# Pool columns of the input projection: one 512- and one 256-column product per block instead of three of 256

## The chip, the cores and the metric

The kernel runs on one core of a Trainium2 chip. The metric is the device time of one execution in microseconds; the median of three runs is compared.

## The reference

One layer of a decoder trunk on 256 tokens of width 2048, all in float32. Cut to what matters here:

```
h   = rmsnorm(x)
z   = h @ w_in          # pool channels (1024) | q | k | v | indexer q | indexer k | indexer weights
A   = pool_mixer(u_pool)        # 4 groups of 256 channels, causal means over 2/4/8/16 tokens
B   = dsa_attention(q, k, v, q_idx, k_idx, w_idx)     # 64 best keys per query, softmax attention
x1  = x + concat(A, B) @ w_out
out = x1 + conv_ffn(rmsnorm(x1))

pool_mixer:  d = (mean over the last w tokens) - u, for each group
             y = (d @ pool_w[group]) * pool_scale
```

## The kernel before

Every float32 number that TensorE multiplies is split in two: a high half (the value rounded to TensorE's format) and a low half (what is left). A product of two float32 matrices is then high x high, high x low and low x high, and low x low is left out. The tile xhl holds the normalised input, feature by feature, as [128, block, half, 256 tokens], so high and low half of one block lie side by side; whi and wlo hold the two halves of 1024 weight columns of the 128 partitions.

The work is a list of *pieces*, each of them 1024 weight columns: a DMA on SyncE's queue brings a unit of two pieces (tile raw), ScalarE rounds to whi (L103), VectorE subtracts to wlo (L104), TensorE runs the piece's products. There are four buffers of whi and of wlo, so a piece's split waits for the piece four earlier. The pieces come in the order of ORDER: the indexer chunks (24 pieces), k0 and k1, u0, q0 and q1, u1, v0, u2, v1, u3, then the output projection (32), the up projection (176) and the down projection (88). A chunk u0 to u3 is a pool chunk: four pieces, for two tiles of 128 pool columns, and its window is 16, 8, 4 and 2 in that order.

There are three forms of product in which the weights are stationary and 256 tokens move. With a rhs of both halves, mm_feat (L216, L217) streams high and low half in one product of 512 columns against whi, and the high half once more against wlo; its accumulator has 512 columns, and low half's sum lies in columns 256 to 511. mm_feat1 (L221 to L223) runs three products of 256 columns that all add into columns 0 to 255. The up projection and most of the down projection use mm_feat; pool chunks, the pool mixer, the output projection and the last two tiles of the down projection use mm_feat1. The query, key, value and indexer chunks use the other form, mm_tok (L210 to L212), with the weights moving.

Accumulators of a chunk come from a pool of two, each of two banks of 512 columns; a chunk holds its accumulator from its first product until it has been taken out.

Work beside the pieces is hung on steps of the list with at(step, ...): at a step, first the split of the piece two further on, then the side work of the step, then the products of the step's own piece. For pool chunk n with its first piece at step f, the weights of the mixer are loaded and split at f - 2 and f + 2, pool_u (L541 to L545) takes the accumulator out at f + 4, pool_win (L547) computes the window sums on VectorE and the two halves dhl (ScalarE L566, VectorE L567), and pool_mix multiplies by pool_w. For the first three chunks pool_win hangs on step f + 5 and pool_mix on f + 10; for the last on f + 4 and f + 6. So between the last chunk and its mixer TensorE has two pieces of the output projection and two attention outputs (L529, L530, taken out by L531 and L532). The framework's planner sets the final order on each engine: instructions come in the order of the program, but one that is ready in the planner's own times can go ahead of one that is not.

The up projection's accumulators are taken out by up_out (L635 to L637): ScalarE copies the columns 256 to 511, VectorE adds the columns 0 to 255 and multiplies by the token norm.

Of the kernel before, what the change touches and what calls it, by code (L numbers as in the profile page):

```python
# [11 lines left out]
AF = mybir.ActivationFunctionType  # L12
ALU = mybir.AluOpType
AX = mybir.AxisListType

P = 128
S = 256
D = 2048
KT = D // P
# [24 lines left out]
def hybrid_kernel(ctx, tc, xT, par, wIa, wIb, wIc, wI2, wA, wU, wP, wO, wUp, wDn, out):  # L44
    nc = tc.nc
# [9 lines left out]
    xhl = cp.tile([P, KT, 2, S], F32R, name="xhl")  # L55
# [114 lines left out]
    r1, r2 = TokenNorm("r1"), TokenNorm("r2")  # L170
# [43 lines left out]
    def mm_feat(o, wh, wl, rhs, first, last):  # L214

        nc.tensor.matmul(o, wh, rhs.rearrange("p a t -> p (a t)"), start=first, stop=False)  # L216
        nc.tensor.matmul(o[:, 0:S], wl, rhs[:, 0], start=False, stop=last)  # L217

    def mm_feat1(o, wh, wl, rhs, first, last):

        nc.tensor.matmul(o[:, 0:S], wh, rhs[:, 0], start=first, stop=False)  # L221
        nc.tensor.matmul(o[:, 0:S], wh, rhs[:, 1], start=False, stop=False)  # L222
        nc.tensor.matmul(o[:, 0:S], wl, rhs[:, 0], start=False, stop=last)  # L223
# [13 lines left out]
    def pool_chunk(n):  # L237
        acc = Acc()
        for j in range(2):
            u = Unit(wU[2 * n + j], D)  # L240
            for h in range(2):
                def mm(p, j=j, h=h):
                    pt = acc.get()
                    for i in range(8):
                        k = 8 * h + i
                        mm_feat1(pt[:, j], *p.get(i * P, P), xhl[:, k], k == 0, k == KT - 1)
                pieces.append(Piece(u, h * 1024, (h + 1) * 1024, mm))
        return acc

# [287 lines left out]
    def wide(name):  # L537
        return zc.tile([P, 2, S + 16], F32, name=name, tag="t2", bufs=5)

    def pool_u(n):  # L540
        pt = ua[n].get()  # L541
        ub = wide("ub")
        nc.gpsimd.memset(ub[:, :, 0:16], 0.0)
        nc.vector.tensor_tensor(ub[:, :, 16:], pt[:, :, 0:S], r1.b2(), op=ALU.mult)
        pw_[n] = ub  # L545

    def pool_win(n):  # L547
# [161 lines left out]
    for n in range(4):  # L709
        st = first[f"u{n}"] + 4  # L710
        at(st, pool_u, n)
        at(st - 6, pool_w, n)
        at(st - 2, pool_ws, n)
        at(st + (n < 3), pool_win, n)
        at(st + 2 + 4 * (n < 3), pool_mix, n)
# [112 lines left out]
```

## Time and profile before

| | us |
|---|---|
| median of three runs | 1098.67 (1098.51 to 1098.75) |
| the profiled execution | 1098.5 |
| its span in the trace | 1096.8 |
| TensorE busy | 1090.8 |
| VectorE busy | 729.8 |
| ScalarE busy | 569.7 |

The span runs from the first to the last instruction in the trace, and the profiled execution took 1.7 us more than its span. Engines are listed with the time in which at least one of their instructions ran. TensorE's matmuls overlap, and their ends are modelled, so the distance between two starts tells more of a product than its listed duration. A weight split is one ScalarE instruction of about 1.06 us and one VectorE instruction of about 1.23 us.

### The profile page before, as it was taken

How to read it: one execution, taken by the hardware profiler on the slowest of the kernel's cores; microseconds unless marked ns; L12 is line 12 of the kernel's file. 1: busy time of each engine (PE TensorE's matmuls, PEld its weight loads, DVE VectorE, ACT ScalarE, POOL GpSimd, SP SyncE). 2: the span in 40 equal slices, each digit the busy share in tenths (PEclk: the TensorE clock that was granted, in tenths of full speed). 3: DMA queues.
4: the chain of work that ended last, by engine and by line, in shares of the span. 5: the costliest groups of instructions: out<-in, count | busy, mean ns of one | idle time of the engine just before them, and what ended most of it. 6: DMA issues, size and time to landing. Idle time of an engine off the chain costs nothing.

```text
span 1096.8 us, 16441 instructions
## 1 busy us (share of the span) xinstructions
PE 1090.8 (99%) x6620; PEld 973.5 (89%) x6620; DVE 729.8 (67%) x1037; ACT 569.7 (52%) x796; POOL 13.8 (1%) x25
## 2 busy tenths in 40 slices
PE   9999999999999999999999999999999999999998
PEld 7988889889999888888888888888888888888898
DVE  7667857665565687777777777777787544444442
ACT  7555456654444555555555555555555443333441
POOL 0001000000000000000000000000000000000000
PEclk9999999999999999999999999999999999999999
DMA  8554564444555555555555555555555556555552
GB/s 289 169 188 148 178 231 156 164 163 154 171 180 189 192 192 192 189 184 192 186 189 183 191 191 192 188 192 192 192 192 192 193 201 201 197 195 198 195 197 74
DMA packets 31755, 204.30 MB, mean 186 GB/s; under 512 B 3648, under 2 KB 4288, under 8 KB 8640
## 3 DMA queue, kind: packets, MB, share of 16 engines
q1 hardware_dynamic: 30240, 201.16, 53.7%
q10 hardware_dynamic: 1440, 2.11, 0.5%
q8 instruction: 52, 0.85, 0.3%
q14 instruction: 23, 0.19, 0.0%
HBM read 201.15 MB, written 2.10 MB: 185 GB/s over the span
## 4 chain that ended last, share of the span: by engine, by line
PE 99%; DMA 1%; SPq 0%; ACT 0%; DVE 0%; issue 0%; ACTq 0%
PE mm L216 43%; PE mm L217 21%; PE mm L210 5%; PE mm L212 5%; PE mm L211 5%; PE mm L221 5%; PE mm L222 5%; PE mm L223 5%; PE sp L403 1%; DMA xf<-in_xT_dram 1%; PE sp L489 0%; PE tp L477 0%; PE op L529 0%; PE tp L517 0%; PE tp L393 0%; PE pm L221 0%
## 5 line engine op out<-in xcount | busy, mean ns | idle before, releaser
L104 DVE TENSOR_TENSOR wlo<-raw,whi 128x1024 fp32r<-128x1024 f32 (+4 forms) x385 | 462.6, 1203 | 296.2 <-ACT whi L103 294.9
L103 ACT ACTIVATE whi<-raw 128x1024 fp32r<-128x1024 f32 (+4 forms) x385 | 399.9, 1041 | 429.4 <-PE mm L216 262.4
L216 PE MATMUL mm<-xhl,whi 128*128 128x512 f32 x1408 | 488.4, 394 | 0.0
L217 PE MATMUL mm<-xhl,wlo 128*128 128x256 f32 x1408 | 390.1, 277 | 0.0
L216 PEld LDWEIGHTS mm<-xhl,whi 128*128 128x128 f32 x1408 | 264.0, 187 | 61.0
L217 PEld LDWEIGHTS mm<-xhl,wlo 128*128 128x128 f32 x1408 | 264.4, 188 | 0.0
L216 PE MATMUL mm<-ghl,whi 128*128 128x512 f32 x616 | 213.6, 394 | 0.0
L217 PE MATMUL mm<-ghl,wlo 128*128 128x256 f32 x616 | 170.6, 277 | 0.0
L216 PEld LDWEIGHTS mm<-ghl,whi 128*128 128x128 f32 x616 | 115.5, 188 | 26.8
L217 PEld LDWEIGHTS mm<-ghl,wlo 128*128 128x128 f32 x616 | 115.7, 188 | 0.0
L210 PE MATMUL mm<-whi,xhl 128*128 128x512 f32 (+3 forms) x288 | 108.3, 376 | 1.1 <-ACT xhl L120 0.5
L212 PE MATMUL mm<-whi,xhl 128*128 128x512 f32 (+3 forms) x288 | 106.8, 371 | 0.0
L211 PE MATMUL mm<-wlo,xhl 128*128 128x512 f32 (+3 forms) x288 | 106.6, 370 | 0.2 <-DVE wlo L104 0.2
L221 PE MATMUL mm<-yhl,whi 128*128 128x256 f32 x256 | 72.2, 282 | 0.0
L223 PE MATMUL mm<-yhl,wlo 128*128 128x256 f32 x256 | 72.1, 281 | 0.0
L222 PE MATMUL mm<-yhl,whi 128*128 128x256 f32 x256 | 72.1, 281 | 0.0
L210 PEld LDWEIGHTS mm<-whi,xhl 128*128 128x128 f32 x288 | 54.1, 188 | 9.0 <-issue 0.9
L212 PEld LDWEIGHTS mm<-whi,xhl 128*128 128x128 f32 x288 | 54.1, 188 | 8.3 <-DVE xhl L123 0.5
L211 PEld LDWEIGHTS mm<-wlo,xhl 128*128 128x128 f32 x288 | 54.1, 188 | 7.3 <-DVE wlo L104 0.4
L654 ACT ACTIVATE ghl<-fc 128x256 fp32r<-128x256 f32 x44 | 18.4, 417 | 57.8 <-DVE fc L653 57.8
L221 PEld LDWEIGHTS mm<-yhl,whi 128*128 128x128 f32 x256 | 48.2, 188 | 0.0
L222 PEld LDWEIGHTS mm<-yhl,whi 128*128 128x128 f32 x256 | 48.2, 188 | 0.0
(156 smaller groups left out, 955.6 us busy)
## 6 DMA issues: line engine op xcount, KB each, us to landing
raw<-in_wUp_dram SPq DMA_DIRECT2D x88, 1024.0 KB, 4.8
raw<-in_wDn_dram SPq DMA_DIRECT2D x44, 1024.0 KB, 4.8
raw<-in_wA_dram SPq DMA_DIRECT2D x24, 1024.0 KB, 4.8
raw<-in_wO_dram SPq DMA_DIRECT2D x16, 1024.0 KB, 4.8
raw<-in_wU_dram SPq DMA_DIRECT2D x8, 1024.0 KB, 5.0
raw<-in_wI_dram SPq DMA_DIRECT2D x4, 640.0 KB, 4.0
raw<-in_wIb_dram SPq DMA_DIRECT2D x3, 784.0 KB, 4.5
xf<-in_xT_dram SPq DMA_DIRECT2D x8, 256.0 KB, 4.9
```

Source lines behind the costliest of these rows:

```text
L103: i1 = nc.scalar.activation(hi, raw, AF.Copy)
L104: i2 = nc.vector.tensor_tensor(self.lo[:, c:c + n], raw, hi.bitcast(F32), op=ALU.subtract)
L210: nc.tensor.matmul(o, xhl[:, k, 0, t], wh, start=(k == 0), stop=False)
L211: nc.tensor.matmul(o, xhl[:, k, 0, t], wl, start=False, stop=False)
L212: nc.tensor.matmul(o, xhl[:, k, 1, t], wh, start=False, stop=(k == KT - 1))
L216: nc.tensor.matmul(o, wh, rhs.rearrange("p a t -> p (a t)"), start=first, stop=False)
L217: nc.tensor.matmul(o[:, 0:S], wl, rhs[:, 0], start=False, stop=last)
L221: nc.tensor.matmul(o[:, 0:S], wh, rhs[:, 0], start=first, stop=False)
L222: nc.tensor.matmul(o[:, 0:S], wh, rhs[:, 1], start=False, stop=False)
L223: nc.tensor.matmul(o[:, 0:S], wl, rhs[:, 0], start=False, stop=last)
L403: nc.tensor.matmul(sp[:, a:b], q, kiT[:, e, 0:b - a], start=(e == 0), stop=(e == 1))
L654: nc.scalar.activation(ghl[:, f, 0], c[:, 0], AF.Copy)
```

## The change

The pool chunks call mm_feat in place of mm_feat1, so a block takes one product of 512 and one of 256 columns, and the accumulator has the low half's sum in columns 256 to 511. pool_u therefore has two more instructions ahead of the multiplication by the token norm: ScalarE copies the columns 256 to 511 into the tile ub, and VectorE adds the columns 0 to 255 to it; the multiplication then works on ub in place.

```diff
@@ -243,7 +243,7 @@
                     pt = acc.get()
                     for i in range(8):
                         k = 8 * h + i
-                        mm_feat1(pt[:, j], *p.get(i * P, P), xhl[:, k], k == 0, k == KT - 1)
+                        mm_feat(pt[:, j], *p.get(i * P, P), xhl[:, k], k == 0, k == KT - 1)
                 pieces.append(Piece(u, h * 1024, (h + 1) * 1024, mm))
         return acc
 
@@ -541,7 +541,10 @@
         pt = ua[n].get()
         ub = wide("ub")
         nc.gpsimd.memset(ub[:, :, 0:16], 0.0)
-        nc.vector.tensor_tensor(ub[:, :, 16:], pt[:, :, 0:S], r1.b2(), op=ALU.mult)
+        uv = ub[:, :, 16:]
+        nc.scalar.activation(uv, pt[:, :, S:2 * S], AF.Copy)
+        nc.vector.tensor_tensor(uv, pt[:, :, 0:S], uv, op=ALU.add)
+        nc.vector.tensor_tensor(uv, uv, r1.b2(), op=ALU.mult)
         pw_[n] = ub
```

## Rows read from the trace of the kernel before

**Rows 1.** The page: busy time by engine, granted TensorE clock, chain that ended last.

```profile
PE 1090.8 (99%) x6620; PEld 973.5 (89%) x6620; DVE 729.8 (67%) x1037; ACT 569.7 (52%) x796; POOL 13.8 (1%) x25
...
PEclk9999999999999999999999999999999999999999
...
PE 99%; DMA 1%; SPq 0%; ACT 0%; DVE 0%; issue 0%; ACTq 0%
```

**Rows 2.** Busy time by stretch: stretch, its us, each engine's busy us, clock, DMA.

```profile
8.90:1093.30 1084.40, 1084.24 (x6600) 970.51 (x6600) 725.80 (x1029) 565.74 (x790) 12.05 (x14) 1.00 0.55 186
...
123.45:139.00 15.55, 15.55 (x71) 12.88 (x70) 13.57 (x18) 6.55 (x7) 0.00 (x0) 1.00 0.57 201
```

**Rows 3.** Products by line: count, ns (least/median/most), first and last start, forms.

```profile
L216 PE MATMUL mm<-xhl,whi x1408: 391/392/476, 359.1 to 847.7; 128*128 128x512 f32 x176
...
L216 PE MATMUL mm<-ghl,whi x616: 392/394/395, 848.1 to 1061.3; 128*128 128x512 f32 x154
...
L221 PE MATMUL mm<-yhl,whi x256: 279/281/363, 265.7 to 358.7; 128*128 128x256 f32 x128
...
L221 PE MATMUL mm<-ghl,whi x88: 280/283/283, 1061.6 to 1092.9; 128*128 128x256 f32 x88
...
L221 PE MATMUL pm<-dhl,pwh x16: 279/283/283, 139.8 to 273.3; 128*128 128x256 f32 x16
```

**Rows 4.** TensorE in order of time around the first pool chunk: start, us, instruction.

```profile
111.72 0.39 PE L212 MATMUL mm<-whi,xhl 128*128 128x512 f32 x1
111.94 0.28 PE L221 MATMUL mm<-xhl,whi 128*128 128x256 f32 x1
...
123.45 0.40 PE L210 MATMUL mm<-whi,xhl 128*128 128x512 f32 x1
```

**Rows 5.** Groups by line and form: count, busy us, mean ns, idle before.

```profile
L637 DVE TENSOR_TENSOR up<-ft,r2b 128x512 f32<-128x512 f32 x44 | 30.4, 692 | 1.5
L636 DVE TENSOR_TENSOR ft<-mm,ft 128x512 f32<-128x512 f32 x44 | 30.1, 684 | 0.0
L635 ACT ACTIVATE ft<-mm 128x512 f32<-128x512 f32 x44 | 25.4, 577 | 0.0
...
L544 DVE TENSOR_TENSOR ub<-mm,r1b 128x512 f32<-128x512 f32 x4 | 2.8, 690 | 1.6 <-PE mm L223 1.6
```

**Rows 6.** VectorE in order of time after the first pool chunk.

```profile
126.25 0.68 DVE L544 TENSOR_TENSOR ub<-mm,r1b 128x512 f32<-128x512 f32 x1
...
131.13 1.23 DVE L104 TENSOR_TENSOR wlo<-raw,whi 128x1024 fp32r<-128x1024 f32 x1 [0.92 <-ACT whi L103]
...
135.72 0.69 DVE L567 TENSOR_TENSOR dhl<-d,dhl 128x512 fp32r<-128x512 f32 x1 [0.70 <-ACT dhl L566]
```

**Rows 7.** VectorE, then ScalarE, in order of time after the last pool chunk.

```profile
265.37 0.69 DVE L544 TENSOR_TENSOR ub<-mm,r1b 128x512 f32<-128x512 f32 x1 [0.60 <-PE mm L223]
...
266.81 0.42 DVE L532 TENSOR_TENSOR yhl<-op,yhl 128x256 fp32r<-128x256 f32 x1
...
267.81 1.22 DVE L104 TENSOR_TENSOR wlo<-raw,whi 128x1024 fp32r<-128x1024 f32 x1
...
269.80 0.69 DVE L567 TENSOR_TENSOR dhl<-d,dhl 128x512 fp32r<-128x512 f32 x1 [0.70 <-ACT dhl L566]
...
265.25 1.06 ACT L103 ACTIVATE whi<-raw 128x1024 fp32r<-128x1024 f32 x1 [1.99 <-PE mm L222]
266.21 0.36 ACT L531 ACTIVATE yhl<-op 128x256 fp32r<-128x256 f32 x1
```

**Rows 8.** TensorE in order of time, from the last pool chunk past its mixer.

```profile
265.05 0.28 PE L223 MATMUL mm<-xhl,wlo 128*128 128x256 f32 x1
...
272.31 0.28 PE L222 MATMUL pm<-dhl,pwh 128*128 128x256 f32 x1
...
273.62 0.28 PE L221 MATMUL mm<-yhl,whi 128*128 128x256 f32 x1
```

**Rows 9.** Waits: engine and line, for what, us in total, times, longest us.

```profile
ACT zq L445 <- PE mm L212: 3.1, 2, 1.7
```

## The prediction

> **What bounds the kernel now.** The page comes first: busy shares, granted clock, chain of waits [rows 1]. TensorE is busy 1090.8 us of a 1096.8 us span, the chain that ended last is TensorE to 99%, and the granted clock reads full speed in all 40 slices, so the 2.4 GHz level is not at stake. Busy time can deceive, because matmuls overlap, so the second view is the busy time by stretch [rows 2]: between 8.90 and 1093.30 us TensorE leaves 0.16 us open, and the 6.0 us of idle lie nearly all at the start and the end. The kernel is a queue of products with no gap. Its time changes by what the change takes out of that queue, plus any gap that it opens; vector work counts only where it opens one.
>
> VectorE does not bound the kernel, but it is close in one of the stretches that the change touches: 13.57 us busy of 15.55 us after the first pool chunk [rows 2]. So the third view is the order of instructions around the points where a pool accumulator is taken out.
>
> **The change on TensorE.** Four pool chunks of two column tiles by 16 blocks make 128 blocks. Each now takes three 256-column products, and will take a 512- and a 256-column one. Columns stay at 768; one product, with its weight load, goes. What a product costs is the distance from start to start, not its duration, since the listed durations overlap.
> - Three products on pool blocks: the first chunk runs 32 blocks from 111.94 to 123.45 us with nothing between [rows 4], 359.7 ns each. The last stage does the same on another tile: 88 blocks with first starts from 1061.6 to 1092.9 us [rows 3], 31.3 / 87 = 359.8 ns.
> - Two products, 512 + 256: 1408 blocks of the up projection start at 359.1 us, and the next stage's first at 848.1 [rows 3], 489.0 / 1408 = 347.3 ns. The down projection, 616 blocks from 848.1 to 1061.3: 213.2 / 615 = 346.7 ns.
> - A third stage gives a lower price for three products: the output projection's last 240 blocks start from 273.62 [rows 8] to 358.7 us [rows 3], 85.1 / 239 = 356 ns.
>
> The same tile pair (xhl, whi) gives 359.7 - 347.3 = 12.4 ns a block, the final stage 359.8 - 346.7 = 13.1 ns, the cheapest triple against the dearer pair 356 - 347.3 = 8.7 ns. Times 128 that is 1.6, 1.7 and 1.1 us. I take **1.6 us off the queue**, because it is from the loop that is changed and from the form that it gets, and keep 1.1 and 1.7 as bounds. The trace has both forms at the same granted clock, so there is no reason for a value outside by the clock.
>
> **The change on ScalarE and VectorE.** Per chunk, ScalarE gains one copy out of the accumulator, the same shape as the copy in the up projection: 577 ns [rows 5]. VectorE gains one addition out of the accumulator, 684 ns, and its multiplication now reads SBUF: 692 ns against 690 ns now [rows 5], taken as nothing. So four times 0.58 us on ScalarE and 0.68 us on VectorE, and the window work of a chunk starts at least 0.58 + 0.68 = 1.26 us later. The 5.0 us of vector work are nothing if TensorE never finds a buffer empty. Chunk by chunk:
> - First chunk. VectorE reaches the multiplication at 126.25 us, 2.7 us after the chunk's last product started; that is time for the copy. The addition pushes VectorE's queue 0.68 us back, but VectorE stands idle 0.92 us for ScalarE before the split at 131.13 [rows 6], which takes that up. Cost 0; without that idle stretch it would push the end of the mixer's input from 135.72 + 0.69 = 136.41 us [rows 6] to 137.1, still ahead of the mixer's first product at 139.8 [rows 3].
> - Second and third chunk. The mixer runs six pieces after the chunk, as in the first: at least 15.8 us, a piece of 12 products being 12 times the 0.22 us that a 512-column product holds the queue [rows 4]. The chain from taking out to mixer input was 10.2 us in the first chunk (126.25 to 136.41 [rows 6]), which has the most window steps. Cost 0; the chain would have to grow by some 5 us first.
> - Last chunk. Only two pieces lie between it and its mixer, so here is **the one tight place**. The last product starts at 265.05 [rows 8]; the vector chain starts at 265.37 and ends with the mixer's low half at 269.80 + 0.69 = 270.49 [rows 7]. TensorE's first product that reads that half starts at 272.31 [rows 8]. The cover is 1.8 us against at least 1.26 us more: it holds by half a microsecond if the copy starts at once. It may not. ScalarE begins a weight split at 265.25 and follows it with an attention output [rows 7], so the copy may start near 266.5 and end near 267.05. Then VectorE would do the split and the attention subtraction first (they stand inside the chain now, at 267.81 and 266.81, 1.13 and 0.33 us of it), and the addition would start near 267.9. From there the chain is its own work: 0.65 for the addition, 0.65 multiplication, 0.7 window, 0.65 difference, 0.25 for the two fixes, 0.7 ScalarE, 0.7 the last subtraction, that is about 272.2, on the edge. One more weight split in the gap before the last subtraction (VectorE is free there for 0.7 us) makes it 273.0 and a stall of 0.7 us. The order on each engine is set by a planner, whose own times the trace does not show, so I bound the stall by 0 and 0.8 us and take **0.3 us**, nearer to the first end because only one of the orders gives it.
>
> **Buffers.** The accumulator is held 1.26 us longer or more. There are two; the next chunk has the other one, and the one after that starts eight pieces later, or four after the last chunk: from 273.62 to 265.05 [rows 8] are already 8.6 us, and the next use is later still. Cost 0. The copy writes into a tile whose border GpSimd had cleared long before; no DMA moves.
>
> **The sum.** 1096.8 - 1.6 + 0.3 = 1095.5 us of span. The profiled execution took 1098.5, 1.7 us more than its span, which stays: 1097.2. The median of the three runs is 0.17 above that execution, which makes 1097.4, or 1.3 us (0.12%) less than 1098.67.
>
> **Rivals.**
> 1. *The chain of the last chunk outruns its cover, and the kernel gets slower.* Price: each microsecond of delay past 1.8 us is one of TensorE idle at 272.3 us. It eats the gain from a delay of 3.4 us on (1.8 + 1.6), and passes the 0.2% bound (2.2 us, about what a measurement of this kernel can tell from no change) from 5.6 us on. Place: the copy starts 1.1 us late (266.5 instead of 265.37), the addition waits for a split and an attention subtraction, the last subtraction for another split. All of it with nothing given back, 1.26 + 1.1 + 1.13 + 0.33 + 1.13 = 5.0 us, would be a stall of 3.2 us and 1098.67 - 1.6 + 3.2 = 1100.3 us. Against it: one split and the subtraction stand in the chain already and are not added by the change, and TensorE has a further piece on other data that the planner can set there. A ScalarE queue that waits for TensorE holds back what stands behind it; the copies out of the query accumulators wait up to 1.7 us for TensorE [rows 9], with splits behind them, and TensorE shows no gap there. The Trainium skill, page "TensorE: Matmul & The Clock Gate", the table of specifications, has ScalarE and VectorE as strict first-in-first-out queues of 8, a rule that speaks against an additional copy on ScalarE; the trace agrees that ScalarE waits, but not that it costs, since the splits are ahead by whole pieces.
> 2. *The saved product was free.* If the 13 ns that a product costs beyond its columns belonged to the reading of the operands and not to the product, two products would cost the pool blocks what three do: 1098.7 us, give or take 0.3. For it, only that the three rows for triples differ by 4 ns with what is read. Against it, both forms stand in the trace on the same tiles. Working: 359.8 ns less 768 columns at 2.4 GHz (320 ns) is 39.8, 13.3 a product; the pair's 346.7 - 320 = 26.7 is 13.3 a product too. By the Trainium skill, the same page, section "Back-to-back issue gap", a warm product costs its columns and 2.5 ns, which would make the gain 128 x 2.5 = 0.3 us and the kernel 1098.4 us; the rows here say 13.3.
> 3. *The planner sets much else in another order.* It weighs all instructions anew, so attention and weight splits between 120 and 280 us could change places. In this stretch TensorE had no gap to win back, so it can only lose there: 1097 to 1099.5 us. A real gain past 2.2 us would need 17 ns a block, more than a whole product's overhead.
>
> **How the numbers follow.** Forecast, gain 1.1 to 1.7 us with a stall of 0 to 0.8: 1096.9 to 1098.5, likeliest 1097.4, chance 0.70. Rival 1: 0.12, of which 0.04 past the bound. Rival 2: 0.06. Rival 3: 0.12, of which 0.02 past the bound on the slow side. Something no row shows that makes it more than 0.2% faster: inside these, 0.04. So faster 0.04, same 0.90, slower 0.06. The range reaches 0.4 us under the forecast's low end, for a scatter of the runs of 0.2 us and a pair a little cheaper than in the rows, and up through most of rival 1 and 3: 1096.5 to 1099.3.
>
> **What would show it.** Right: 128 products fewer of 256 columns from the pool chunks and 128 of 512 more; the first chunk's 32 blocks take 11.1 us, not 11.5; the up projection starts 1.3 to 1.7 us earlier; TensorE's waits gain at most one row, at a mixer product near 272 us. Wrong: a TensorE wait over 1 us on the mixer's input or on a split; pool blocks at 355 ns or more; or anything from the up projection on that changes its length, since nothing is touched there.

## The result, and where the 12.5 us went

The changed kernel takes 1111.18 us (1111.08 to 1111.44 in four runs) against 1098.67, a ratio of 1.0115 (95% interval 1.0099 to 1.0131). It is **slower by 12.5 us**; 1.3 us less had been forecast. The profiled execution's span grew from 1096.8 to 1109.5 us.

The page of the kernel after, the same three lines as [rows 1]: busy time by engine, granted clock, chain.

```profile
PE 1104.4 (100%) x6492; PEld 974.1 (88%) x6492; DVE 733.0 (66%) x1041; ACT 571.5 (52%) x800; POOL 13.7 (1%) x25
...
PEclk9999999999999999999999999999999999999999
...
PE 98%; DVE 1%; DMA 0%; ACT 0%; issue 0%; SPq 0%; ACTq 0%; DVEq 0%
```

TensorE has 128 products fewer, is still busy all the time at full clock, and is busy 13.6 us longer. So no engine holds it up: its products themselves take longer. Which ones shows in the view of products by line of the kernel after, which answers to [rows 3]:

```profile
L216 PE MATMUL mm<-xhl,whi x1536: 389/398/582, 111.9 to 856.3; 128*128 128x512 f32 x192
...
L216 PE MATMUL mm<-ghl,whi x616: 395/398/403, 856.6 to 1073.9; 128*128 128x512 f32 x154
...
L221 PE MATMUL mm<-ghl,whi x88: 281/283/283, 1074.3 to 1105.6; 128*128 128x256 f32 x88
```

and in the order of time on TensorE around the first pool chunk and at the start of the up projection:

```profile
111.93 0.39 PE L216 MATMUL mm<-xhl,whi 128*128 128x512 f32 x1
...
123.22 0.40 PE L210 MATMUL mm<-whi,xhl 128*128 128x512 f32 x1
...
358.37 0.40 PE L216 MATMUL mm<-xhl,whi 128*128 128x512 f32 x1
```

By stage, from start to start:

| stage | before us | after us | difference |
|---|---|---|---|
| first pool chunk to up projection | 111.94 to 359.1 | 111.93 to 358.37 | -0.7 |
| up projection, 1408 pairs | 848.07 - 359.06 = 489.0 | 856.65 - 358.37 = 498.3 | +9.3 |
| down projection, 616 pairs | 1061.62 - 848.07 = 213.55 | 1074.31 - 856.65 = 217.66 | +4.1 |
| last two tiles, 87 starts | 31.3 | 31.3 | 0 |

The stretch that the change touches did give back a little. The loss lies wholly in the up and down projections, where the change alters nothing: in the two built programs, the 4366 TensorE instructions from the up projection on have the same order, the same operands and the same addresses. A pair of 512 and 256 columns takes 217.66 / 616 = 353.3 ns there, where it took 213.55 / 616 = 346.7. The instructions of line L216 alone in 100 us of the up projection (stretch, its us, TensorE busy with the count of products, weight loads, clock, DMA), first in the kernel after, then in the one before:

```profile
400.00:500.00 100.00, 100.00 (x284) 53.18 (x283) 1.00 0.54 184
```

```profile
400.00:500.00 100.00, 100.00 (x289) 54.10 (x289) 1.00 0.56 190
```

The same form ran at the lower price too, in the same execution. TensorE in order of time in the first chunk of the up projection of the kernel after, before and after the four one-column products of the token norm (L152), and then around its second group (L163) and later:

```profile
362.25 0.40 PE L216 MATMUL mm<-xhl,whi 128*128 128x512 f32 x1
...
363.31 0.40 PE L216 MATMUL mm<-xhl,whi 128*128 128x512 f32 x1
...
364.03 0.50 PE L152 MATMUL pc<-ones,sq 128*128 128x1 f32 x4
...
364.82 0.40 PE L216 MATMUL mm<-xhl,whi 128*128 128x512 f32 x1
...
365.86 0.39 PE L216 MATMUL mm<-xhl,whi 128*128 128x512 f32 x1
...
370.02 0.61 PE L163 MATMUL pb<-dg,ones 128*128 128x128 f32 x4
...
499.79 0.40 PE L216 MATMUL mm<-xhl,whi 128*128 128x512 f32 x1
...
500.85 0.40 PE L216 MATMUL mm<-xhl,whi 128*128 128x512 f32 x1
```

In each case the two rows are three pairs apart: 1.06 us (353 ns a pair) ahead of the first group, 1.04 us (347 ns) behind it, and 1.06 us again behind the second, from where on nothing breaks into the row for 700 us. That gave the theory for the experiments. **Theory A:** the starts of a long row of products settle into one of two repeating patterns, and the moment at which other products last broke into the row decides which. **Theory B:** something lasting that the change brought (the vector work, the accumulator's use, the count of instructions) makes every later pair dearer.

### The profile page after: what moved, and what is told of

Same layout as the page of the kernel before. It is cut to its first block, busy times and chain, and to the rows that moved or that the text cites. A ratio compares the mean times of both kernels' runs of the same rounds, so it can differ in the third digit from the quotient of the medians.

```text
span 1109.5 us, 16197 instructions
## 1 busy us (share of the span) xinstructions
PE 1104.4 (100%) x6492; PEld 974.1 (88%) x6492; DVE 733.0 (66%) x1041; ACT 571.5 (52%) x800; POOL 13.7 (1%) x25
## 4 chain that ended last, share of the span: by engine, by line
PE 98%; DVE 1%; DMA 0%; ACT 0%; issue 0%; SPq 0%; ACTq 0%; DVEq 0%
PE mm L216 46%; PE mm L217 23%; PE mm L210 5%; PE mm L212 5%; PE mm L211 5%; PE mm L223 4%; PE mm L222 4%; PE mm L221 3%; PE sp L403 1%; PE sp L489 0%; DMA raw<-in_wIa_dram 0%; PE tp L477 0%; ACT whi L103 0%; DVE wlo L104 0%; PE tp L517 0%; PE tp L393 0%
## 5 line engine op out<-in xcount | busy, mean ns | idle before, releaser
L104 DVE TENSOR_TENSOR wlo<-raw,whi 128x1024 fp32r<-128x1024 f32 (+4 forms) x385 | 462.6, 1203 | 305.4 <-ACT whi L103 304.1
L216 PE MATMUL mm<-xhl,whi 128*128 128x512 f32 x1536 | 544.2, 399 | 0.0
L217 PE MATMUL mm<-xhl,wlo 128*128 128x256 f32 x1536 | 431.2, 281 | 0.0
L216 PEld LDWEIGHTS mm<-xhl,whi 128*128 128x128 f32 x1536 | 288.6, 188 | 71.4
L217 PEld LDWEIGHTS mm<-xhl,wlo 128*128 128x128 f32 x1536 | 290.1, 189 | 0.2
L216 PE MATMUL mm<-ghl,whi 128*128 128x512 f32 x616 | 217.7, 399 | 0.0
L217 PE MATMUL mm<-ghl,wlo 128*128 128x256 f32 x616 | 173.0, 281 | 0.0
L216 PEld LDWEIGHTS mm<-ghl,whi 128*128 128x128 f32 x616 | 115.7, 188 | 29.0
L221 PE MATMUL mm<-yhl,whi 128*128 128x256 f32 x256 | 72.2, 282 | 0.0
L221 PEld LDWEIGHTS mm<-yhl,whi 128*128 128x128 f32 x256 | 48.2, 188 | 0.0
L223 PEld LDWEIGHTS mm<-yhl,wlo 128*128 128x128 f32 x256 | 48.2, 188 | 0.0
```

Of the source, the lines that this page charges most:

```text
L104: i2 = nc.vector.tensor_tensor(self.lo[:, c:c + n], raw, hi.bitcast(F32), op=ALU.subtract)
```

## Experiments

A time that stands without a range or an interval is that of a single execution. 346.7 ns a pair is called the cheap price or pattern here, 353.3 ns the dear one.

**A survey.** 42 small products were set into the up projection, one in the middle of each chunk from the third on, from 64 to 105 columns wide; what they compute is never read. Once with the change, once without.

```diff
+    def kick(n):
+        pk = ps_s.tile([P, 512], F32, name="pk", tag="ss")
+        nc.tensor.matmul(pk[:, 0:n], warm[:, 0:P], warm[:, 0:n], start=True, stop=True)
...
+    for f in range(2, NF):
+        at(G0 + 4 * f + 2, kick, 62 + f)
```

> The kernel after the change, with one more small product (64 to 105 columns, one more column each time, its result never read) in the middle of each of 42 chunks of the up projection. Theory A (pattern): the starts of the products settle into one of at least two repeating patterns, 346.7 and 353.3 ns for a pair of 512 and 256 columns, and which one depends on the moment at which other products last broke into the row. Then pairs change price only at the small products, some stretches of 32 pairs come out near 346.7 and some near 353.3 ns, and the whole lies between 1100 and 1115 us (42 small products cost 0.07 us each, 3 us). Theory B (standing cause: the added copy and addition, the accumulator's use, or the number of instructions makes every later pair dearer): all stretches stay at 353.3 ns, 1114 us.

> The same small products in the kernel before the change. Theory A: some stretches of 32 pairs go to about 353.3 ns without any part of the change being there, 1102 to 1115 us in all. Theory B: all stretches stay at 346.7 ns, 1098.7 + 3 = 1102 us.

With the change 1113.58 us, without it 1113.8 us. The small products in order of time; from one to the next there are 32 pairs. First with the change, then without:

```profile
387.62 0.20 PE L677 MATMUL pk<-warm 128*128 128x64 bf16 x1
398.86 0.20 PE L677 MATMUL pk<-warm 128*128 128x65 bf16 x1
410.28 0.20 PE L677 MATMUL pk<-warm 128*128 128x66 bf16 x1
421.71 0.20 PE L677 MATMUL pk<-warm 128*128 128x67 bf16 x1
432.93 0.20 PE L677 MATMUL pk<-warm 128*128 128x68 bf16 x1
444.36 0.20 PE L677 MATMUL pk<-warm 128*128 128x69 bf16 x1
```

```profile
387.81 0.21 PE L674 MATMUL pk<-warm 128*128 128x64 bf16 x1
399.05 0.20 PE L674 MATMUL pk<-warm 128*128 128x65 bf16 x1
410.47 0.20 PE L674 MATMUL pk<-warm 128*128 128x66 bf16 x1
421.90 0.20 PE L674 MATMUL pk<-warm 128*128 128x67 bf16 x1
433.12 0.20 PE L674 MATMUL pk<-warm 128*128 128x68 bf16 x1
```

The distances are 11.24, 11.42, 11.43, 11.22 and 11.43 us, and the same four in the kernel without the change. Two values and none between. Over all starts in the trace, without the first pairs behind a small product, the pairs of a stretch took 346.5 to 346.7 ns behind 14 of the 42 and 353.0 to 353.6 behind the others, in the same 14 places in both kernels. The price never changed inside a stretch, and the two kernels, which had come to the first small product at 353 and at 347 ns, went alike from it on. (A small product cost 0.12 to 0.15 us, 11.24 - 32 x 0.3467 for one, not the 0.07 that was expected.) So the dear price needs no part of the change, and the change doesn't forbid the cheap one. Theory B falls as a cause by itself.

**The two parts alone.** First the vector work with the products of before, then the products with the accumulator taken out as before.

```diff
+        uv = ub[:, :, 16:]
+        nc.scalar.activation(uv, pt[:, :, 0:S], AF.Copy, scale=0.0)
+        nc.vector.tensor_tensor(uv, pt[:, :, 0:S], uv, op=ALU.add)
+        nc.vector.tensor_tensor(uv, uv, r1.b2(), op=ALU.mult)
```

> The kernel before with the added vector work alone: three products of 256 columns as before, but ScalarE copies the accumulator's columns 0 to 255 times zero into ub, VectorE adds the accumulator to it and multiplies in place. Theory B with the vector work as cause: pairs of the up projection at 353.3 ns, 1112 us. Theory A: the vector work costs nothing by itself, apart from at most 0.8 us at the last pool mixer; 1098.7 to 1099.5 us if the pattern of the up projection stays, 1112 us only if the mixer's wait shifts the moment at which the up projection's pattern is set.

> The change's products alone: 512 and 256 columns a pool block, but the accumulator is taken out by the one multiplication as before, so the sum in columns 256 to 511 is left out. Theory B with the vector work as cause: 1097 us. Theory B with the products or their count as cause: 1111 us. Theory A: 1097 or 1111 us, by the pattern after the token norm's last products in the up projection; before these the pool chunks give back 1 to 1.7 us.

The vector work alone: 1112.4 us. The products alone: 1097.46 us, 1.2 less than before. By these two runs alone one would have blamed the vector work; the survey and the runs below speak against that. The down projection's first products by line, vector work alone, then products alone:

```profile
L216 PE MATMUL mm<-ghl,whi x616: 395/398/403, 857.9 to 1075.2; 128*128 128x512 f32 x154
```

```profile
L216 PE MATMUL mm<-ghl,whi x616: 392/394/395, 847.0 to 1060.2; 128*128 128x512 f32 x154
```

217.3 / 615 = 353.3 ns and 213.2 / 615 = 346.7 ns. Of the 14.9 us between the two kernels, 13.4 arise from the up projection on and are the pattern; the rest arises ahead of it.

**One small product with the change, two without.** If theory A holds, the loss can be taken away and made at will.

```diff
+    at(G0 + 10, kick, 64)              # in the kernel after
...
+    for f in (2, 3):                   # in the kernel before
+        at(G0 + 4 * f + 2, kick, 62 + f)
```

> The whole change, and one product of 64 columns (its result never read) in the third chunk of the up projection, where it turned the pairs from 353.3 to 346.7 ns in the survey. Theory A (pattern): 1944 pairs after it at 346.7 instead of 353.3 ns, 13.0 us less, so 1111.2 - 13.0 + 0.1 = 1098.3 us. Theory B (the added vector work makes every later pair dearer): 1111.3 us.

> The kernel before with the survey's first two small products alone, 64 and 65 columns, in the third and fourth chunk of the up projection; no part of the change. Theory A: the second one leaves the pairs at 353.4 ns as in the survey, for 1912 pairs, 12.7 us: 1111.5 us. Theory B: 1098.8 us.

With the change and one 64-column product: 1098.74 us, a ratio of 1.0000 to before (0.9991 to 1.0009). Without the change and with two small products: 1111.99 us, where the kernel before took 1098.86 beside it. One small product removed the whole loss of the change, and two of them made a loss of the same size, 13.1 us, in the kernel that had none. The down projection by line, with the change and one product, then without the change and two:

```profile
L216 PE MATMUL mm<-ghl,whi x616: 391/391/391, 848.0 to 1061.2; 128*128 128x512 f32 x154
```

```profile
L216 PE MATMUL mm<-ghl,whi x616: 395/398/403, 857.4 to 1074.7; 128*128 128x512 f32 x154
```

**The change in part of the chunks.** Here the question was what shifts the moment, and TensorE's wait at the last pool mixer was my candidate.

```diff
-mm_feat(pt[:, j], ...)
+(mm_feat if n < 3 else mm_feat1)(pt[:, j], ...)      # n == 3 in the other kernel; pool_u likewise
```

> The change on the first three pool chunks alone, products and vector work; the last chunk, two pieces ahead of its mixer, as before. Theory A, with the last mixer's delay as the step that shifts the moment: TensorE's order and waits around the last mixer are those of before, the up projection keeps 346.7 ns, and the three chunks give back some 0.8 us: 1097.8 us. Theory B (vector work or 512-column products in themselves): 1111 us or a good part of it.

> The change on the last pool chunk alone. Theory A, with the last mixer's delay as the step that shifts the moment: TensorE waits 0.3 us at the mixer as with the whole change, the up projection goes to 353.3 ns, 1098.7 + 13.3 = 1112 us. If the four chunks together are needed: 1098.5 to 1099 us.

The first three chunks: 1098.02 us, ratio 0.9992 (0.9983 to 1.0002), the down projection at 346.7 ns. Three quarters of the vector work cost nothing, as argued. The last chunk alone: 1099.78 us, and **my candidate failed**. TensorE waits at the mixer just as with the whole change, but the up and down projections kept the cheap pattern. The wait and the down projection of the last chunk alone:

```profile
PEld pm L221 <- ACT dhl L572: 0.3, 1, 0.3
...
L216 PE MATMUL mm<-ghl,whi x616: 392/394/395, 849.3 to 1062.5; 128*128 128x512 f32 x154
```

What it lost lies in the output projection, 80 us of which (line L221 alone) count 223 blocks of three products:

```profile
276.00:356.00 80.00, 62.40 (x223) 42.26 (x223) 1.00 0.53 185
```

In the kernels before and after, the same view counts 226. So the form with three products has two patterns as well. From start to start the blocks behind the mixer took (359.98 - 275.02) / 236 = 360.0 ns here and (358.71 - 273.62) / 239 = 356.0 in the kernel before, on the same operands.

**The mixer one step later.** The reverse of the last: the whole change, but no wait.

```diff
-        at(st + 2 + 4 * (n < 3), pool_mix, n)
+        at(st + 3 + 3 * (n < 3), pool_mix, n)
```

> The whole change, with the last pool mixer one step (a piece of the output projection) later and the first three one step earlier or as before, so that TensorE does not come to the last mixer before its input. What it tells apart: whether TensorE's wait there is the step that set off the dear pattern. Expected under that: no TensorE wait on dhl, the up projection at 346.7 ns a pair, 1098.7 - 1.2 = 1097.5 us. If the moment falls badly for another reason: 353.3 ns and 1110.8 us; the wait would then not be needed for it.

> The same, with the one 64-column product in the third chunk of the up projection, after which the pairs ran at 346.7 ns in three of three kernels, whatever they had been before. Expected: 346.7 ns from there on in any case, 1097.6 us if the pairs ahead of it are at 346.7 too, 1098 us if not; 0.6 to 1.3 us less than the kernel before.

1110.8 us (1110.59 to 1111.20), ratio 1.011, with no wait on dhl left in the trace; the first products of pool and up projection are 357.76 - 111.66 = 246.10 us apart, 0.3 less than with the wait. (The first three mixers kept their step.) With the small product added, 1098.43 us, ratio 0.9998 (0.9988 to 1.0007): 0.5 us less than the kernel before beside it, not clear of noise, where 0.6 to 1.3 had been expected. The down projection by line without the small product, then with it:

```profile
L216 PE MATMUL mm<-ghl,whi x616: 395/398/403, 856.0 to 1073.3; 128*128 128x512 f32 x154
```

```profile
L216 PE MATMUL mm<-ghl,whi x616: 391/391/391, 848.0 to 1061.2; 128*128 128x512 f32 x154
```

The wait is neither needed for the dear pattern (here) nor enough for it (last chunk alone). What remains of the candidate is only that whatever moves TensorE's products ahead of the up projection, by a wait or by another order, can move the outcome. The 64-column product left the cheap pattern behind it in all five kernels in which it stood, whether the pairs ahead of it had been dear (three) or cheap (two). Of the versions with the whole computation the first three chunks (1098.02) and this one (1098.43) have the lowest medians, and neither is clear of the kernel before.

**Where the outcome was settled.** The traces of all these kernels narrow theory A down. Three pairs ahead of the token norm's first group took 1.06 us in the kernel after, as shown above; these are three in the kernel before:

```profile
362.19 0.39 PE L216 MATMUL mm<-xhl,whi 128*128 128x512 f32 x1
...
363.23 0.39 PE L216 MATMUL mm<-xhl,whi 128*128 128x512 f32 x1
```

They took 1.04 us. In all twelve kernels (seven different programs up to there) the sixteen pairs ahead of the first group had the price that the row took behind the second one, and all twelve ran cheap between the two. So the token norm's products did not decide the outcome: it was there at the first pairs of the up projection. In the programs of before and after, TensorE's instructions agree in order, operands and addresses not only from there on but already from the output projection's last 237 blocks on, which took 356.0 ns a block in both. What differs is what stands ahead of these, and so how many blocks of the output projection follow the mixer's last product. The count of line L221 in that stretch, before, after, and with the change on the last chunk alone:

```profile
273.60:359.05 85.45, 67.53 (x240) 45.09 (x240) 1.00 0.51 173
```

```profile
273.99:358.36 84.37, 66.69 (x237) 44.51 (x237) 1.00 0.51 175
```

```profile
275.00:360.30 85.30, 66.60 (x237) 44.93 (x237) 1.00 0.50 173
```

The products alone and the first three chunks have 240, as before, and are cheap; the vector work alone has 238 and the mixer one step later 234, and both are dear, as is the change with 237. The last chunk alone is cheap with 237, and there the blocks took 360.0 ns. So it fits the runs that the change reached the up projection by its vector work, which delays the mixer's input and so had the planner set blocks of the output projection ahead of the mixer's last product. No run changes that count alone, so this is argued and not shown.

What stays open: why TensorE has two patterns for the same row, and why it holds them. The traces show starts of products and nothing of what sets them.

## The prediction, step by step

**What bounds the kernel** was right: TensorE's queue without a gap, before and after.

**The gain on TensorE** was taken as 12.4 ns on each of 128 blocks, 1.6 us. The products alone gave 1.0 us from the first pool product to the up projection: 247.1 us before, 246.1 there and in the kernel with the mixer later; with the wait the change kept 0.7. 1.0 us is 7.8 ns a block, and just under the lower bound of 1.1 us. The term was too large because the pool's new pairs ran at the dear price in part: the first chunk 123.22 - 111.93 = 11.29 us for 32, 352.8 ns, not 347.3, and the other three were dear in their first half. The 11.1 us that were named as the sign of the step did not come.

**The vector work** was right for the first three chunks: the copy took 578 ns and the addition 684, and the chunks hid them. (The first chunk's last product started 2.9 us ahead of 126.25, not 2.7; nothing hangs on it.) At the last chunk the walk gave a copy from 266.5 us, an addition near 267.9, the mixer's input complete at 272.2 to 273.0 and a stall of 0.3 us. The rows of the kernel after, ScalarE, then VectorE, then TensorE, and the wait:

```profile
265.47 0.59 ACT L545 ACTIVATE ub<-mm 128x512 f32<-128x512 f32 x1
...
266.82 0.68 DVE L546 TENSOR_TENSOR ub<-mm,ub 128x512 f32<-128x512 f32 x1
...
268.97 0.42 DVE L532 TENSOR_TENSOR yhl<-op,yhl 128x256 fp32r<-128x256 f32 x1
...
269.97 1.22 DVE L104 TENSOR_TENSOR wlo<-raw,whi 128x1024 fp32r<-128x1024 f32 x1
...
271.96 0.69 DVE L570 TENSOR_TENSOR dhl<-d,dhl 128x512 fp32r<-128x512 f32 x1 [0.70 <-ACT dhl L569]
...
264.05 0.28 PE L217 MATMUL mm<-xhl,wlo 128*128 128x256 f32 x1
...
271.98 0.51 PE L221 MATMUL pm<-dhl,pwh 128*128 128x256 f32 x2
...
272.79 0.30 PE L222 MATMUL pm<-dhl,pwh 128*128 128x256 f32 x1
...
PEld pm L221 <- ACT dhl L569: 0.3, 1, 0.3
```

The chunk's last product started at 264.05 us, 1.0 earlier than before, so 1.0 us is to be added to these rows to set them beside the walk. The copy (266.5) and the addition (267.8) came as walked. The low half was complete at 271.96 + 0.69 = 272.65, on the walk's clock 273.65, later than its latest: an attention subtraction (L532) and a weight split (L104) stood inside the chain once more, 272.2 + 0.33 + 1.13 = 273.66. Before, TensorE wanted that half 272.31 - 265.05 = 7.26 us behind the chunk's last product; at that distance it would have come at 271.31 and waited 1.3 us, past the bound of 0.8 (an estimate from these rows). It lost only 0.3 us, waiting for the high half that ScalarE writes (dhl L569): the planner had set nine more products of the output projection (three blocks) ahead of and between the mixer's, and these covered the rest. Rival 1 had named that way out. So the chain was mis-sized, and the 0.3 us is right by luck.

**The step that failed** is in the part on TensorE and in the sum: a pair of 512 and 256 columns was given one price, 346.7 to 347.3 ns, and 1096.8 - 1.6 + 0.3 carried the up and down projections over at their old length, "since nothing is touched there". They took 13.4 us more, some 2000 pairs at 6.7 ns more, ten times the 1.3 us that had been forecast. That the clock gives no reason for another price was right, the granted clock stayed at 1.00; the price changed at the same clock. Rival 3, another order by the planner, was the right place to look. Its price, up to 1099.5 us, was wrong, because it counted only what TensorE could lose between 120 and 280 us.

The rows to see it by were there. The form of three products had two prices in the trace of before, 359.7 and 356 ns [rows 3, 4, 8], and rival 2 put that down to what is read. The last-chunk kernel shows the output projection at the other price on the same operands. A product's cost beyond its columns at 2.4 GHz, 13.3 ns in the prediction, is (353.3 - 320) / 2 = 16.7 in the dear pattern. The Trainium skill, page "TensorE: Matmul & The Clock Gate", section "Back-to-back issue gap", gives the 2.5 ns for a single product by itself and not for a row of weight loads and products, which the prediction left out; they fit neither pattern. **Rival 1** (a stall past the gain) did not come: 0.3 us. The last sign named for being wrong, a length that changes from the up projection on, is the one that appeared.

## What to carry to other kernels

Take the price of a form from several stretches, start to start; where one trace shows the same form at two prices, ask what a later stage costs at the other one, and put that into the range, even for a change that is far from that stage. After a change, compare first the stages that it does not touch; if they changed length with TensorE gapless at full clock, look for the place where the price switches. Before a small loss or gain is put down to the work that was added, break the row once with one small product: a loss that goes away with it is not work that every later product pays for. A loss that stays shows nothing, since 28 of the 42 small products left the dear price behind them.

## What the runs showed of the hardware

A gapless row of pairs of 512 and 256 columns (32-bit operands, full granted clock) ran at 346.7 or at 353.3 ns a pair, with identical instructions and addresses, and kept its price for as long as nothing broke in, over 1900 pairs in a row. A foreign product of 64 to 105 columns could switch it either way, and the same width set at the same place gave the same outcome in both kernels. A break need not decide for good: in all twelve kernels the row ran cheap for the sixteen pairs between the token norm's two groups, and behind the second took the price again that it had had ahead of the first. Blocks of three 256-column products show two prices as well, 356 and 360 ns. The changed kernel's runs repeat within 0.4 us nonetheless (1111.08 to 1111.44), so a repeated measurement doesn't show that the outcome hangs on this.
